# Down projection: 18 of 22 block pairs in the seven-product form, with all their weight sums made ahead and five pairs' activation forms kept in device memory

## The chip, the cores and the metric

The kernel runs on one core of a Trainium2 chip. The metric is device microseconds of one execution. A core has five engines that run side by side, each with its own queue of instructions: TensorE (PE in the profile; its weight loads are PEld), VectorE (DVE), ScalarE (ACT), GpSimd (POOL) and SyncE (SP). They meet at semaphores. Data come from device memory by DMA; a DMA is issued from the queue of SP, ACT or POOL and is then carried by the core's 16 DMA engines. TensorE reads SBUF and adds into PSUM, which VectorE and ScalarE read.

## What is computed

One decoder layer in float32 with 256 tokens and a model width of 2048: a mixer of three kinds of heads, a projection, and a gated feed-forward part with 5632 features. The change touches the last line only, the product with `w_down`:

```python
def conv_glu_ffn(h, w_gate, w_up, conv_w, conv_b, w_down):
    g = h @ w_gate                                  # [256, 5632]
    gp = jnp.pad(g, ((0, 0), (CONV_WIDTH - 1, 0), (0, 0)))
    gc = conv_b
    for j in range(CONV_WIDTH):
        gc = gc + conv_w[j] * gp[:, j:j + S]
    return (jax.nn.silu(gc) * (h @ w_up)) @ w_down  # [256, 5632] @ [5632, 2048]

x = x + conv_glu_ffn(rms_norm(x, g_ffn), w_gate, w_up, conv_w, conv_b, w_down)
```

## The kernel before

**High and low parts.** TensorE multiplies floats rounded to a shorter format (F32R). To keep float32 accuracy every operand is split: ScalarE writes the rounded high part (`wh`, line 101), VectorE the rest (`wl`, line 102), both in `split_w`, into rings of four buffers each. A product is then three matmuls: high x high, low x high, high x low (`prod`, lines 906 to 910).

**Gate and up.** The 5632 features are 44 blocks of 128 (`f`). For each f the loop at line 879 loads one block of `w_gate` and one of `w_up` (1 MB each, line 88, a ring of three buffers named `wr`), splits them and multiplies them with the normed tokens `h2`: 96 matmuls of 256 columns (line 165). `glu` (lines 824 to 854) then makes the gated feature block: convolution, silu, product.

**Down.** Two neighbouring feature blocks are a pair `j`; there are 22. The outputs are computed in two halves `c` of 1024 columns. For a half, a pair of feature blocks, two blocks of 128 tokens and two of 512 columns make a 2 x 2 by 2 x 2 block product. A *plain* pair does it with eight block products, 24 matmuls of 512 columns (`plain`). A *seven* pair uses a scheme with seven block products, 21 matmuls (`seven`): its activations are seven sums of the four blocks, made in `glu` and kept as a tile `aS` of seven high and seven low parts (128 x 14 x 128), and its weights are three blocks and four sums of blocks. Three of the seven products go to accumulators of one output block each (`own`), four to accumulators of common parts (`com`), which `common` and `finish` put together at the end of a half and add to the residual.

**Where the weight sums are made.** `KIND` at line 43 gives each place of the order a letter. "p" is plain (8 of 22). "s" (6) is a seven pair whose sums VectorE makes in down, one pair ahead (`make_sums`, lines 928 to 938). "S" (8) is a seven pair whose sums are made during gate and up: `presum` (lines 859 to 866) loads the four weight blocks through the same ring `wr`, makes four differences on VectorE and stores the result to device memory (`tsum`) from POOL's queue. There are 16 such jobs, one for each half and "S" pair, one behind each odd f from 3 to 33. In down an "S" pair loads three quarters of its weights in two pieces, and 1 MB of sums.

**Queues.** All loads of weights are issued in program order from SP's queue: a load that waits for its buffer holds back those behind it. In down the loads use four places in turn, the ring of three and a part of `dn` (line 900). POOL's queue issues the stores of the sums, the loads of the residual `x1s` into `dn` (line 967) and the first half's output.

Of the kernel before, what the change touches and what calls it, by code (L numbers as in the profile page):

```python
# [18 lines left out]
P = 128  # L19
# [19 lines left out]
NN = 512  # L39

PAIRS = KF // 2
ORDER = tuple(range(PAIRS - 3)) + (PAIRS - 1, PAIRS - 2, PAIRS - 3)
KIND = "pSspSsSpsSpSspSsSpsSpp"
SEVEN = tuple(j for j, k in zip(ORDER, KIND) if k != "p")
SUMMED = tuple((c, j) for c in range(2) for j, k in zip(ORDER, KIND) if k == "S")

VEC = [
    ("g_mix", KD), ("g_ffn", KD), ("g_q_lat", QR // P), ("g_kv_lat", KVR // P),
# [15 lines left out]
def layer(ctx, tc, xT_d, xn_d, memT_d, vec_d, tab_d, w_z_d, w_mqkr_d, w_q_d, w_kv_d, w_mem_d, w_pool_d, w_o_d,  # L64
# [10 lines left out]
    def nm(s):  # L75
        uid[0] += 1
        return f"{s}_{uid[0]}"
# [13 lines left out]
    def keep(ins, on=True):  # L91

        return tc.keep_in_program_order(ins) if on else ins
# [730 lines left out]
    def glu(f, psg, psu, home=None):  # L824
        g = fp.tile([P, T], F32, tag="g", name=nm("g"), bufs=1)
        nc.vector.tensor_tensor(g[:], psg, r1[:], op=ALU.mult)  # L826
        gc = fp.tile([P, T], F32, tag="gc", name=nm("gc"), bufs=1)
        nc.scalar.activation(gc[:], g[:], AF.Identity, bias=v("conv_b", f), scale=v("cw2", f))  # L828
        for d, w in ((1, "cw1"), (2, "cw0")):
            nc.vector.scalar_tensor_tensor(gc[:, d:T], g[:, 0:T - d], v(w, f), gc[:, d:T], op0=ALU.mult, op1=ALU.add)  # L830
        nc.scalar.activation(gc[:], gc[:], AF.Silu)  # L831
        j, e = f // 2, f % 2
        if j not in SEVEN:
            if e == 0:
                aT[j] = fp.tile([P, 2, 2 * T], F32R, name=nm("aT"))
            nc.vector.tensor_tensor(gc[:], psu, gc[:], op=ALU.mult)
            split_act(aT[j][:, e, :], gc[:])
            return
        if e == 0:
            aT[j] = home if j == PAIRS - 1 else fp.tile([P, 14, P], F32R, name=nm("aS"))[:]  # L840
            hold[j] = fp.tile([P, 8, P], F32, tag="s8", name=nm("s8"), bufs=1)
        elif home is not None:
            aT[j] = home
        s = hold[j]
        o = 0 if e else 6
        nc.vector.tensor_tensor(s[:, o:o + 2, :].rearrange("p a t -> p (a t)"), psu, gc[:], op=ALU.mult)
        if e:
            for d, a, op, b in ((2, 7, ALU.add, 1), (3, 2, ALU.subtract, 6), (4, 6, ALU.subtract, 7),
                                (5, 0, ALU.subtract, 3)):
                nc.vector.tensor_tensor(s[:, d, :], s[:, a, :], s[:, b, :], op=op)  # L850
            hi, lo = (aT[j][:, i:i + 7].rearrange("p a t -> p (a t)") for i in (0, 7))
            sf = s[:, 0:7, :].rearrange("p a t -> p (a t)")
            nc.scalar.copy(hi, sf)
            nc.vector.tensor_tensor(lo, sf, hi.bitcast(F32), op=ALU.subtract)


    tsum = dp.tile([P, len(SUMMED), STG], F32, name="tsum")

    def presum(i):

        raw = load_w(w_dn_d[SUMMED[i]], STG)
        r = raw.rearrange("p (b n) -> p b n", n=NN)
        for d, a, b in ((0, 1, 0), (1, 2, 1), (2, 2, 0), (3, 3, 2)):
            nc.vector.tensor_tensor(r[:, d], r[:, a], r[:, b], op=ALU.subtract)  # L864
        for h in range(2):
            nc.gpsimd.dma_start(tsum[:, i, h * HS:(h + 1) * HS], raw[:, h * HS:(h + 1) * HS])  # L866
# [12 lines left out]
    for f in range(1, KF):  # L879
        pss = [ps_main()[:, 0:T] for _ in range(2)]  # L880
        gemm_pair(pss, [load_w(w[f], STG) for w in (w_g_d, w_u_d)], h2)
        if f < KF - 1:
            glu(f, *pss)
        if f % 2 and 3 <= f < 3 + 2 * len(SUMMED):
            presum(f // 2 - 1)

# [5 lines left out]
    dn = big.tile([P, 12, NN], F32, tag="act", name="dn")  # L892
    aS = big.tile([P, 14, P], F32R, tag="act2", name="aS")
    glu(KF - 1, *pss, aS[:])
    cnt = [0, 0]

    def load_dn(src, parts=((0, STG),)):

        cnt[1] += 1
        raw = dn[:, 4:8].rearrange("p b n -> p (b n)") if cnt[1] % 4 == 0 else stage.tile(  # L900
            [P, STG], F32, tag="wr", name=nm("wr"), bufs=3)[:]
        for a, b in parts:
            nc.sync.dma_start(raw[:, a:b], src[:, a:b])
        return raw

    def prod(ps, a, b, first, last):
# [5 lines left out]
    def plain(c, j, own, first, last, kept, between=None, by_bank=False):  # L912
        raw = load_dn(w_dn_d[c, j])
        ws = [split_w(raw, 0, HS, kept=kept)]
        if between is not None:
            between()
        ws.append(split_w(raw, HS, HS, kept=kept))
        order = [(k, t, n) for k in range(2) for t in range(NT) for n in range(2)]
        if by_bank:
            order.sort(key=lambda o: o[1:])  # L920
        for k, t, n in order:
            a = [aT[j][:, k, o + t * P:o + (t + 1) * P] for o in (0, T)]
            s = n if k == 0 else 1 - n
            prod(own[t, n], a, [w[:, s * NN:(s + 1) * NN] for w in ws[k]], first and k == 0, last and k == 1)

    ready = {}

    def make_sums(c, j):

        raw = load_dn(w_dn_d[c, j])  # L930
        r3 = raw.rearrange("p (b n) -> p b n", n=NN)
        i = cnt[0] % 2
        cnt[0] += 1
        f13, f24 = dn[:, 2 * i:2 * i + 2], dn[:, 2 - 2 * i:4 - 2 * i]
        keep(nc.vector.tensor_tensor(f13, r3[:, 1:3], r3[:, 0:2], op=ALU.subtract))
        keep(nc.vector.tensor_tensor(f24[:, 0], r3[:, 2], f13[:, 0], op=ALU.subtract))
        keep(nc.vector.tensor_tensor(f24[:, 1], r3[:, 3], f24[:, 0], op=ALU.subtract))
        ready[c, j] = (raw, *(f.rearrange("p b n -> p (b n)") for f in (f13, f24)))

    def seven(c, j, own, com, first, last, kept, between):  # L940
        if (c, j) in SUMMED:
            raw = load_dn(w_dn_d[c, j], ((0, NN), (2 * NN, STG)))
            sums = load_dn(tsum[:, SUMMED.index((c, j))])
            F13, F24 = sums[:, 0:HS], sums[:, HS:STG]
        else:
            raw, F13, F24 = ready.pop((c, j))
        b11 = split_w(raw, 0, NN, kept=kept)
        b2 = split_w(raw, 2 * NN, HS, kept=kept)
        if between is not None:
            between()  # L950
        t13 = split_w(F13, 0, HS, kept=kept)
        t24 = split_w(F24, 0, HS, kept=kept)
        for (b, s), f, ps, own_ in (((b11, 0), 6, com[0], False), ((b2, 0), 5, own[0, 1], True),
                                    ((b2, 1), 0, own[0, 0], True), ((t13, 0), 2, com[1], False),
                                    ((t13, 1), 4, com[3], False), ((t24, 0), 3, com[2], False),
                                    ((t24, 1), 1, own[1, 0], True)):
            prod(ps, [aT[j][:, i + f, :] for i in (0, 7)], [w[:, s * NN:(s + 1) * NN] for w in b],
                 first and not own_, last and not own_)

    def common(c, com, step):  # L960

        v1, u2, u3, u5 = (dn[:, i, :] for i in range(4))
        if step == 0:
            for t in range(NT):
                for n in range(2):
                    o = c * HS + n * NN
                    nc.gpsimd.dma_start(dn[:, 8 + 2 * t + n, :], x1s[:, t, o:o + NN])
        elif step == 1:
            keep(nc.scalar.copy(v1, com[0]))
            for u, a, b in ((u2, v1, com[2]), (u3, u2, com[3]), (u5, u3, com[1]), (u2, u2, com[1])):  # L970
# [17 lines left out]
    for c in range(2):  # L988
        own_ps, com_ps = (ps_main, ps_aux) if c else (ps_aux, ps_main)
        own = {(t, n): own_ps()[:] for t in range(NT) for n in range(2)}  # L990
        com = None
        for i, j in enumerate(ORDER):
            kept = c > 0 or i > 1
            between = None
            if i == 0 and done is not None:
                between = lambda o=done: finish(0, o, nc.gpsimd)
            elif i >= PAIRS - 2:
                between = lambda s=i - PAIRS + 3: common(c, com, s)
            elif KIND[i + 1] == "s":
                between = lambda j=ORDER[i + 1]: make_sums(c, j)  # L1000
            if j in SEVEN:
                if com is None:
                    com = [com_ps()[:] for _ in range(4)]
                seven(c, j, own, com, j == SEVEN[0], j == SEVEN[-1], kept, between)
# [8 lines left out]
def _pack(**i):  # L1013
# [58 lines left out]
    r["w_u"] = cols(a["w_up"][0])  # L1072

    w = a["w_down"][0].reshape(PAIRS, 2, P, 2, 2, NN)
    w = np.stack([w[:, 0, :, :, 0], w[:, 0, :, :, 1], w[:, 1, :, :, 1], w[:, 1, :, :, 0]])
    r["w_dn"] = w.transpose(3, 1, 2, 0, 4).reshape(2, PAIRS, P, STG)
    return {n: np.ascontiguousarray(x, dtype=f32) for n, x in r.items()}

# [16 lines left out]
```

## Time and profile before

| | us |
|---|---|
| median of three runs | 998.13 (998.0 to 998.34) |
| the profiled execution | 998.5 |
| its span, first to last instruction | 996.7 |

The profile is of one execution. "Busy" is the time in which an engine had an instruction under way; matmuls are pipelined, so a busy TensorE is not TensorE at its peak. A row of a group of instructions gives the line, the engine, the operation, output<-input by the program's names, the shape, the count, then busy time and the mean ns of one, and the idle time just before them with what ended it. The chain of work that ended last is followed back from the last instruction, at each step to what released it. The granted TensorE clock was 1.00 of full speed throughout.

### The profile page before, as it was taken

The page shows a single profiled execution, that of the slowest core. Times are in us where ns is not written, and L with a number is a line of the kernel's source. Part 1 is how long each engine was busy: PE and PEld are TensorE (multiplying, and loading weights), DVE is VectorE, ACT ScalarE, POOL GpSimd, SP SyncE. Part 2 cuts the span into 40 slices and gives each one's busy share as a digit, 9 for nine tenths or more (in the row PEclk, how much of TensorE's full clock was granted, in tenths as well). Part 3 has the DMA queues.
Part 4 walks back from the last instruction along what each step waited for, and adds up shares of the span by engine and source line. Part 5 has one row for each costly group of instructions (what it writes and reads, how often), then busy time and mean ns, then how long its engine had stood idle before and what let it go on. Part 6 is the DMA issues. An engine that isn't in the chain of part 4 may idle for free.

```text
span 996.7 us, 17150 instructions
## 1 busy us (share of the span) xinstructions
PE 989.7 (99%) x6888; PEld 917.2 (92%) x6888; DVE 757.3 (76%) x1117; ACT 566.2 (57%) x770; POOL 35.5 (4%) x71
## 2 busy tenths in 40 slices
PE   9999999999999999999999999999999999999998
PEld 8899988888889999999999999999999888887886
DVE  6878588765676777777786777876656988898897
ACT  6777665644565554554554455455544666655663
POOL 1100000000000000000000000000000000010000
PEclk9999999999999999999999999999999999999999
DMA  9867445344665888887888887785656877787772
GB/s 359 291 245 287 137 161 178 127 144 145 211 219 190 298 291 296 296 278 288 281 304 291 295 302 276 281 286 182 208 185 207 300 280 273 266 300 284 283 267 102
DMA packets 43296, 246.51 MB, mean 247 GB/s; under 512 B 4944, under 2 KB 5456, under 8 KB 19280
## 3 DMA queue, kind: packets, MB, share of 16 engines
q1 hardware_dynamic: 35424, 218.41, 62.3%
q0 software_dynamic: 7360, 26.22, 6.9%
q8 instruction: 54, 0.88, 0.3%
q10 hardware_dynamic: 432, 0.79, 0.3%
q14 instruction: 26, 0.21, 0.1%
HBM read 224.42 MB, written 20.97 MB: 246 GB/s over the span
## 4 chain that ended last, share of the span: by engine, by line
PE 97%; DVE 1%; ACT 1%; issue 0%; ACTq 0%; DVEq 0%
PE psm L165 47%; PE psm L181 5%; PE psm L182 5%; PE psm L183 5%; PE psm L148 4%; PE psa L910 4%; PE psa L908 4%; PE psa L909 4%; PE psm L908 4%; PE psm L910 4%; PE psm L909 4%; PE psm L132 2%; PE psa L713 1%; PE psa L181 1%; PE psa L183 1%; PE psa L182 1%
## 5 line engine op out<-in xcount | busy, mean ns | idle before, releaser
L102 DVE TENSOR_TENSOR wl<-wr,wh 128x1024 fp32r<-128x1024 f32 (+2 forms) x362 | 419.5, 1168 | 166.7 <-ACT wh L101 110.9
L101 ACT CAST wh<-wr 128x1024 fp32r<-128x1024 f32 (+2 forms) x362 | 362.5, 1006 | 200.5 <-PE psm L165 83.0
L165 PE MATMUL psm<-h,wh 128*128 128x256 f32 x2752 | 319.1, 276 | 0.0
L165 PEld LDWEIGHTS psm<-h,wh 128*128 128x128 f32 x2752 | 315.3, 188 | 0.0
L165 PE MATMUL psm<-h,wl 128*128 128x256 f32 x1376 | 163.0, 276 | 0.0
L165 PEld LDWEIGHTS psm<-h,wl 128*128 128x128 f32 x1376 | 159.2, 188 | 0.0
L101 ACT CAST wh<-dn 128x1024 fp32r<-128x1024 f32 (+1 forms) x54 | 52.6, 974 | 33.3 <-PE psa L909 19.3
L102 DVE TENSOR_TENSOR wl<-dn,wh 128x1024 fp32r<-128x1024 f32 (+1 forms) x54 | 59.6, 1124 | 8.9 <-ACT wh L101 6.9
L828 ACT ACTIVATE gc<-g,vec 128x256 f32<-128x256 f32 x44 | 26.5, 602 | 70.0 <-DVE g L826 70.0
L831 ACT ACTIVATE gc<-gc 128x256 f32<-128x256 f32 x44 | 18.4, 418 | 70.5 <-DVE gc L830 70.5
L864 DVE TENSOR_TENSOR wr<-wr 128x512 f32<-128x512 f32 x64 | 44.1, 689 | 1.1
L830 DVE SCALAR_TENSOR_TENSOR gc<-g,vec,gc 128x255 f32<-128x255 f32 x88 | 42.3, 480 | 1.0
L910 PE MATMUL psa<-wl,aS 128*128 128x512 f32 x98 | 38.4, 392 | 0.9 <-DVE wl L102 0.9
L908 PE MATMUL psa<-wh,aS 128*128 128x512 f32 x98 | 38.2, 389 | 0.0
L909 PE MATMUL psa<-wh,aS 128*128 128x512 f32 x98 | 38.2, 389 | 0.0
L908 PE MATMUL psm<-wh,aS 128*128 128x512 f32 x98 | 38.1, 389 | 0.0
L909 PE MATMUL psm<-wh,aS 128*128 128x512 f32 x98 | 38.1, 389 | 0.0
L910 PE MATMUL psm<-wl,aS 128*128 128x512 f32 x98 | 38.1, 389 | 0.0
L181 PE MATMUL psm<-wh,cat 128*128 128x512 f32 x96 | 38.1, 397 | 0.0
L183 PE MATMUL psm<-wl,cat 128*128 128x512 f32 x96 | 37.4, 390 | 0.0
L182 PE MATMUL psm<-wh,cat 128*128 128x512 f32 x96 | 37.4, 390 | 0.0
L866 POOL DMA_DIRECT2D tsum<-wr x32 | 17.0, 533 | 344.5 <-DVE wr L864 344.5
(233 smaller groups left out, 1362.0 us busy)
## 6 DMA issues: line engine op xcount, KB each, us to landing
wr<-in_w_g SPq DMA_DIRECT2D x44, 1024.0 KB, 5.0
wr<-in_w_u SPq DMA_DIRECT2D x44, 1024.0 KB, 5.5
wr<-in_w_dn SPq DMA_DIRECT2D x37, 1024.0 KB, 5.1
wr<-in_w_o SPq DMA_DIRECT2D x16, 1024.0 KB, 4.9
tsum<-wr POOLq DMA_DIRECT2D x32, 512.0 KB, 4.0
wr<-tsum SPq DMA_DIRECT2D x12, 1024.0 KB, 6.1
wr<-in_w_z SPq DMA_DIRECT2D x10, 1024.0 KB, 6.0
dn<-in_w_dn SPq DMA_DIRECT2D x7, 1024.0 KB, 6.6
```

Source lines behind the costliest of these rows:

```text
L101: keep(nc.scalar.copy(hi[:, c:e], raw[:, o + c:o + e]), kept)
L102: keep(nc.vector.tensor_tensor(lo[:, c:e], raw[:, o + c:o + e], hi[:, c:e].bitcast(F32), op=ALU.subtract), kept)
L148: keep(nc.tensor.matmul(ps, parts[k // nk][low][:, i * P:(i + 1) * P], m, start=k + a == 0 and low == low_first, stop=k == KD - 1 and low ...
L165: nc.tensor.matmul(ps, parts[k // nk][low][:, i * P:(i + 1) * P], m, start=k + a == 0 and low == (s == 1), stop=k == KD - 1 and low == (s ...
L181: keep(nc.tensor.matmul(ps, xh, hi[:, i, o], start=first and i == 0, stop=False), kept)
L182: keep(nc.tensor.matmul(ps, xl, hi[:, i, o], start=False, stop=False), kept)
L183: keep(nc.tensor.matmul(ps, xh, lo[:, i, o], start=False, stop=last and i == nk - 1), kept)
L830: nc.vector.scalar_tensor_tensor(gc[:, d:T], g[:, 0:T - d], v(w, f), gc[:, d:T], op0=ALU.mult, op1=ALU.add)
L864: nc.vector.tensor_tensor(r[:, d], r[:, a], r[:, b], op=ALU.subtract)
L908: nc.tensor.matmul(ps, a[0], b[0], start=first, stop=False)
L909: nc.tensor.matmul(ps, a[1], b[0], start=False, stop=False)
L910: nc.tensor.matmul(ps, a[0], b[1], start=False, stop=last)
```

## The change

The order of the 22 pairs is written out, and only pairs 0, 8, 14 and 15 stay plain. The other 18 are seven pairs, and all of them are summed ahead: 36 jobs instead of 16, spread over f = 2 to 40, one behind each f but 11, 21 and 31 (none). The jobs load into two places of their own (`wj`) instead of the ring `wr`. `make_sums` and `KIND` are gone.

The forms of pairs 16 to 20 (`AWAY`) are not kept in SBUF. They are made in one place (`aL`), stored to device memory (`forms`) from POOL's queue, and in each half loaded back into that one place, one after the other: the next load is issued behind the pair that used the place.

In down the loads go through six places in turn: the three of `wr`, the two of `wj` and the part of `dn`. The first and second weight blocks of a pair are exchanged in the packed weights, so that a seven pair's three blocks are one piece of 768 KB; the signs of two sums and the order of two products follow. The residual's loads move from POOL's queue to SP's, and a plain pair's second block order changes likewise.

```diff
-ORDER = tuple(range(PAIRS - 3)) + (PAIRS - 1, PAIRS - 2, PAIRS - 3)
-KIND = "pSspSsSpsSpSspSsSpsSpp"
-SEVEN = tuple(j for j, k in zip(ORDER, KIND) if k != "p")
-SUMMED = tuple((c, j) for c in range(2) for j, k in zip(ORDER, KIND) if k == "S")
+ORDER = (0, 1, 16, 2, 3, 4, 17, 5, 6, 7, 18, 8, 9, 10, 19, 11, 12, 21, 20, 13, 14, 15)
+PLAIN = (0, 8, 14, 15)
+AWAY = (16, 17, 18, 19, 20)
+SEVEN = tuple(j for j in ORDER if j not in PLAIN)
+SUMMED = tuple((c, j) for c in range(2) for j in SEVEN)
...
-            aT[j] = home if j == PAIRS - 1 else fp.tile([P, 14, P], F32R, name=nm("aS"))[:]
+            aT[j] = (home if j == PAIRS - 1 else away() if j in AWAY
+                     else fp.tile([P, 14, P], F32R, name=nm("aS"))[:])
...
             nc.vector.tensor_tensor(lo, sf, hi.bitcast(F32), op=ALU.subtract)
+            if j in AWAY:
+                nc.gpsimd.dma_start(forms[:, AWAY.index(j)], aT[j])
+
+    forms = dp.tile([P, len(AWAY), 14, P], F32R, name="forms")
+
+    def away():
+        return fp.tile([P, 14, P], F32R, tag="aL", name=nm("aL"), bufs=1)[:]
...
+    def job_place():
+        return fp.tile([P, STG], F32, tag="wj", name=nm("wj"), bufs=2)[:]
...
     def presum(i):
-        raw = load_w(w_dn_d[SUMMED[i]], STG)
+        c, j = SUMMED[i]
+        raw = job_place()
+        nc.sync.dma_start(raw, w_dn_d[c, j])
         r = raw.rearrange("p (b n) -> p b n", n=NN)
-        for d, a, b in ((0, 1, 0), (1, 2, 1), (2, 2, 0), (3, 3, 2)):
+        for d, a, b in ((1, 0, 1), (0, 2, 0), (2, 2, 1), (3, 3, 2)):
...
-        if f % 2 and 3 <= f < 3 + 2 * len(SUMMED):
-            presum(f // 2 - 1)
+        for i in range(len(SUMMED)):
+            if f == 2 + i * (KF - 4) // len(SUMMED):
+                presum(i)
...
+    def load_dn(src, a=0):
+        cnt[0] += 1
+        n = cnt[0] % 6
+        raw = (dn[:, 4:8].rearrange("p b n -> p (b n)") if n == 0 else job_place() if n % 3 == 1
+               else stage.tile([P, STG], F32, tag="wr", name=nm("wr"), bufs=3)[:])
+        nc.sync.dma_start(raw[:, a:STG], src[:, a:STG])
+        return raw
...
+    def fetch(j):
+        aT[j] = away()
+        nc.gpsimd.dma_start(aT[j], forms[:, AWAY.index(j)])
+
+    def seven(c, j, own, com, first, last, kept):
+        raw = load_dn(w_dn_d[c, j], NN)
+        sums = load_dn(tsum[:, SUMMED.index((c, j))])
+        b11 = split_w(raw, NN, NN, kept=kept)
         b2 = split_w(raw, 2 * NN, HS, kept=kept)
+        t31 = split_w(sums, 0, HS, kept=kept)
+        t24 = split_w(sums, HS, HS, kept=kept)
...
-                    nc.gpsimd.dma_start(dn[:, 8 + 2 * t + n, :], x1s[:, t, o:o + NN])
+                    nc.sync.dma_start(dn[:, 8 + 2 * t + n, :], x1s[:, t, o:o + NN])
...
+        rest = [j for j in ORDER if j in AWAY]
+        fetch(rest.pop(0))
         for i, j in enumerate(ORDER):
...
+                seven(c, j, own, com, j == SEVEN[0], j == SEVEN[-1], kept)
+                if j in AWAY and rest:
+                    fetch(rest.pop(0))
...
-    w = np.stack([w[:, 0, :, :, 0], w[:, 0, :, :, 1], w[:, 1, :, :, 1], w[:, 1, :, :, 0]])
+    w = np.stack([w[:, 0, :, :, 1], w[:, 0, :, :, 0], w[:, 1, :, :, 1], w[:, 1, :, :, 0]])
```

More of the change, by code (lines that the diff above doesn't have):

```diff
@@ L894, in layer @@
     glu(KF - 1, *pss, aS[:])
[L895 to L903, printed above, removed]
+    cnt = [0]
+    def load_dn(src, a=0):
[4 more added lines that the diff above has]
+        nc.sync.dma_start(raw[:, a:STG], src[:, a:STG])
         return raw
@@ L922, in plain @@
             a = [aT[j][:, k, o + t * P:o + (t + 1) * P] for o in (0, T)]
-            s = n if k == 0 else 1 - n
+            s = 1 - n
             prod(own[t, n], a, [w[:, s * NN:(s + 1) * NN] for w in ws[k]], first and k == 0, last and k == 1)
[L926 to L947, printed above, removed]
+    def fetch(j):
[5 more added lines that the diff above has]
+        b11 = split_w(raw, NN, NN, kept=kept)
         b2 = split_w(raw, 2 * NN, HS, kept=kept)
[L949 to L952, printed above, removed]
+        t31 = split_w(sums, 0, HS, kept=kept)
+        t24 = split_w(sums, HS, HS, kept=kept)
         for (b, s), f, ps, own_ in (((b11, 0), 6, com[0], False), ((b2, 0), 5, own[0, 1], True),
-                                    ((b2, 1), 0, own[0, 0], True), ((t13, 0), 2, com[1], False),
-                                    ((t13, 1), 4, com[3], False), ((t24, 0), 3, com[2], False),
+                                    ((b2, 1), 0, own[0, 0], True), ((t31, 1), 2, com[1], False),
+                                    ((t31, 0), 4, com[3], False), ((t24, 0), 3, com[2], False),
                                     ((t24, 1), 1, own[1, 0], True)):
@@ L991, in layer @@
         com = None
+        rest = [j for j in ORDER if j in AWAY]
+        fetch(rest.pop(0))
         for i, j in enumerate(ORDER):
             kept = c > 0 or i > 1
[L994 to L1000, printed above, removed]
             if j in SEVEN:
@@ L1003, in layer @@
                     com = [com_ps()[:] for _ in range(4)]
-                seven(c, j, own, com, j == SEVEN[0], j == SEVEN[-1], kept, between)
-            else:
+                seven(c, j, own, com, j == SEVEN[0], j == SEVEN[-1], kept)
+                if j in AWAY and rest:
+                    fetch(rest.pop(0))
+            else:
+                between = None
+                if i == 0 and done is not None:
+                    between = lambda o=done: finish(0, o, nc.gpsimd)
+                elif i >= PAIRS - 2:
+                    between = lambda s=i - PAIRS + 3: common(c, com, s)
                 plain(c, j, own, i == 0, i == PAIRS - 1, kept, between, i == PAIRS - 1)
```

## The prediction

> **What bounds the kernel now.** I read the page's totals first, then its chain of work that ended last, then a table of the stages.
>
> ```profile
> span 996.7 us, 17150 instructions
> PE 989.7 (99%) x6888; PEld 917.2 (92%) x6888; DVE 757.3 (76%) x1117; ACT 566.2 (57%) x770; POOL 35.5 (4%) x71
> ...
> PE 97%; DVE 1%; ACT 1%; issue 0%; ACTq 0%; DVEq 0%
> ```
>
> The chain is TensorE for 97%: only fewer or shorter matmuls can gain, and only as long as nothing else becomes late. The table of stretches (start:end, length, busy us and instruction counts of PE, PEld, DVE, ACT, POOL, then clock, DMA share, GB/s) covers the first loads, gate and up with sums, gate and up without, and down:
>
> ```profile
> 4.00:32.00 28.00, 28.00 (x122) 23.10 (x121) 22.21 (x33) 21.95 (x35) 1.33 (x3) 1.00 1.03 410
> 324.00:650.00 326.00, 326.00 (x2879) 326.00 (x2878) 249.60 (x363) 166.51 (x199) 15.79 (x30) 1.00 0.81 290
> 673.00:747.00 74.00, 74.00 (x655) 74.00 (x655) 46.84 (x65) 37.53 (x48) 0.00 (x0) 1.00 0.56 190
> 770.20:990.90 220.70, 219.79 (x969) 181.18 (x968) 196.72 (x203) 135.62 (x144) 6.34 (x12) 1.00 0.75 265
> ```
>
> Three readings. In down one 512-column matmul costs 219.79/969 = 0.2268 us, and TensorE hardly ever waits. VectorE is at 89% there and 77% in gate and up. The DMA engines move 265 and 290 GB/s, while the first row shows 28 us at 410: that is what they can do when there is always work queued, so about a third is free, and the change will use it.
>
> **The change part by part.** *Matmuls.* A plain pair issues 24 matmuls (two k, two t, two n, three products of high and low parts), a seven pair 7 x 3 = 21. Four pairs in each of two halves change: 8 x 3 = 24 fewer, 24 x 0.2268 = **5.44 us** less. They are on the chain, so this is the whole possible gain but for TensorE's own wait in down, one row:
>
> ```profile
> PE psa L910 <- DVE wl L102: 0.9, 1, 0.9
> ```
>
> *VectorE in down.* The sums of the six "s" pairs in each half leave down. The rows of that stage by shape:
>
> ```profile
> L102 DVE TENSOR_TENSOR wl<-wr,wh 128x1024 fp32r<-128x1024 f32 x70 | 84.2, 1221 | 5.2 <-ACT wh L101 3.9
> L102 DVE TENSOR_TENSOR wl<-wr,wh 128x512 fp32r<-128x512 f32 x17 | 11.6, 685 | 0.0
> L935 DVE TENSOR_TENSOR dn<-wr 128x1024 f32<-128x1024 f32 x6 | 7.3, 1222 | 3.1 <-DMA wr<-in_w_dn 3.1
> L936 DVE TENSOR_TENSOR dn<-wr,dn 128x512 f32<-128x512 f32 x6 | 4.2, 692 | 0.2
> ```
>
> A seven pair's splits cost 3 x 1.221 + 0.685 = 4.35 us of VectorE against 21 x 0.2268 = 4.76 us of TensorE. The 1.22 + 2 x 0.69 = 2.6 us of sums go from twelve pairs, and eight pairs gain 4.35 - 2.44 = 1.9 us each: 31 us out, 15 in. VectorE keeps 91% of a seven pair's time, as now on average, so I cost this at nothing; its cover is the 0.4 us left in each pair, which repays lateness only slowly.
>
> *VectorE in gate and up.* 36 jobs instead of 16, each four of the first row below; before, one in every second feature block f, now one in each f from 2 to 40 except 11, 21 and 31.
>
> ```profile
> L864 DVE TENSOR_TENSOR wr<-wr 128x512 f32<-128x512 f32 x64 | 44.1, 689 | 1.1
> L850 DVE TENSOR_TENSOR s<-s 128x128 f32<-128x128 f32 x53 | 15.4, 291 | 1.4
> L854 DVE TENSOR_TENSOR aS<-s,aS 128x896 fp32r<-128x896 f32 x13 | 14.2, 1093 | 13.2 <-ACT aS L853 13.2
> ...
> 415.93 1.23 DVE L102 TENSOR_TENSOR wl<-wr,wh 128x1024 fp32r<-128x1024 f32 x1 [1.55 <-PE psm L165]
> ```
>
> The row without jobs has 46.84/74 = 63% of VectorE; a job is 2.76 us of the 10.88 us that one f takes, another 25%, and the forms of more pairs 1 or 2%: about 90%. What now falls on the odd f, a job and the end of a pair's forms together, is already in the trace, and there VectorE still idles 1.55 us for TensorE (last line). The change gives the even f a job without the forms. I cost it at nothing too; if the cover goes, each f pays its own tenths, 39 times.
>
> *DMA in gate and up.* The period comes from the timeline of TensorE, and what is loaded or stored from the page's DMA issues (KB each, median us to landing):
>
> ```profile
> 407.51 7.42 PE L165 MATMUL psm<-h,wh 128*128 128x256 f32 x64
> 414.77 3.79 PE L165 MATMUL psm<-h,wl 128*128 128x256 f32 x32
> 418.39 5.83 PE L165 MATMUL psm<-h,wh 128*128 128x256 f32 x50
> ...
> wr<-in_w_g SPq DMA_DIRECT2D x44, 1024.0 KB, 5.0
> tsum<-wr POOLq DMA_DIRECT2D x32, 512.0 KB, 4.0
> wr<-tsum SPq DMA_DIRECT2D x12, 1024.0 KB, 6.1
> wr<-in_w_dn SPq DMA_DIRECT2D x12, 512.0 KB, 4.7
> dn<-x1s POOLq DMA_DIRECT2D x8, 256.0 KB, 7.0
> wr<-in_w_dn SPq DMA_DIRECT2D x12, 256.0 KB, 3.7
> ```
>
> One f is 418.39 - 407.51 = 10.88 us. Two weight blocks are 2.10 MB, a job loads 1.05 and stores 1.05: 4.19 MB, **386 GB/s** wherever a job lies. Over f 32 to 40 four stores of forms (128 x 14 x 128 x 4 bytes = 0.92 MB) come on top: 41.4 MB in 97.9 us, 423 GB/s. The capacity with such a mix, in short stretches of the same table where loads overlap stores (first two rows) and in down (third):
>
> ```profile
> 432.00:436.00 4.00, 4.00 (x38) 4.00 (x37) 3.93 (x6) 2.82 (x3) 1.06 (x2) 1.00 0.98 405
> 455.00:459.00 4.00, 4.00 (x38) 4.00 (x37) 2.92 (x4) 2.78 (x4) 0.53 (x1) 1.00 1.04 372
> 795.00:799.00 4.00, 4.00 (x19) 3.31 (x18) 3.57 (x4) 2.92 (x5) 0.00 (x0) 1.00 0.99 401
> ```
>
> I take 405, near three of the four rows. Then f 2 to 31 just fit (37.7 MB of nine f take 93.2 of 97.9 us) and f 32 to 40 end 41.4/0.405 - 97.9 = 4.3 us late. What covers that is in the queue's timeline:
>
> ```profile
> 408.03 0.33 SPq L88 DMA_DIRECT2D wr<-in_w_g  x1
> ...
> 418.65 0.33 SPq L88 DMA_DIRECT2D wr<-in_w_u  x1
> ...
> 413.46 1.05 ACT L101 CAST wh<-wr 128x1024 fp32r<-128x1024 f32 x1 [1.07 <-DMA wr<-in_w_g]
> ...
> SPq L88 <- DMA tsum<-wr: 24.2, 16, 2.6
> ```
>
> A gate block cast at 413.46 is multiplied from 418.39 + 32 x 0.113 = 422.0: 8.5 us of lead, even where the cast itself waited 1.07 us for the load. The job's own two places (not the weights' ring, as before) take away a wait of the last line's kind, but put another in: SP's load of job i+2 waits for the stores of job i, and the next gate and up loads stand behind it. From VectorE's job end to the next load is some 1 + 4 us, while the job two f later comes 21.8 us on, so this fits. POOL's queue gets 40 more stores, five stores and ten fetches of forms of the 0.53 us that one costs its issuer; it was 4% busy. Cost of the stage: from 0 (405 and all of the lead) to 41.4/0.372 - 97.9 = 13 us less some 6 of lead = 7; I take 1.
>
> *DMA in down.* A seven pair loads 768 KB of blocks and 1,024 KB of sums, 1.835 MB in 4.76 us. One half: 18 x 1.835 + 4 x 1.049 + five forms at 0.92 + 1.05 of residual (its four loads move from POOL's queue into SP's, where they add four issues ahead of the next weights) = 42.9 MB, against 30.4 now. Five of six places and the first forms, 5.6 MB, can be filled before down begins; the first half's output writes 1.05. Left are 2 x 42.9 + 1.05 - 5.6 = 81.1 MB, and they must have landed some 8 us (a plain pair's 5.4 and the first split's 2.3) before the last of 948 x 0.2268 = 215.0 us of matmuls: 81.1/207 = **392 GB/s**. At 401 to 410 it fits with 2 to 4% to spare, at 372 it takes 218 + 8 - 215 = 11 us more. I take 0.5 us.
>
> *Forms fetched.* No row shows a transfer of rounded floats between device memory and SBUF. The single place is free when the last matmul of its pair is done, and the next such pair starts three pairs, 14.3 us, later. The nearest row is four residual loads of 256 KB by POOL's queue beside SP's loads, 7.0 us. At 7 to 10 us it is hidden; that is the value I take. At 20 us each would hold TensorE for some 6 us, ten times.
>
> The sum is made on the profiled execution's 998.5 us (span 996.7 and 1.8 around it): 998.5 - 5.4 + 1.0 + 0.5 = 994.6; the median shown is 0.4 lower, so **994.2**.
>
> A rule of the Trainium skill speaks against this. "DMA: Bandwidth & Descriptors", section Bandwidth, holds that some 358 GB/s of a core's share of device memory binds for loads into SBUF; the "HBM Reference" limits that to both cores of a pair streaming and gives about 425 for one alone. This trace's 410 over 28 us sides with the second.
>
> **The rivals.** *The engines fall short in down (slower).* Mixed sizes, stores and fetches could bring the sustained rate to 380; it decides from 392 down, and beats the gain from 382. Down: 81.1/0.380 + 8 - 215 = 6.4 us; f 32 to 40: 41.4/0.380 - 97.9 = 11, less 6 of lead, 5. 998.1 - 5.4 + 11.4 = 1004. For it: the row of 372, and no stretch over 28 us at 400. Against it: that row holds the start of a transfer after a pause, which a full queue does not have.
>
> *The gain is given back in gate and up alone.* With VectorE at 90% and loads at 96%, a late job load holds VectorE's queue, behind it the low parts. Some 0.1 us in each of 39 f, or the whole 4.3 us of f 32 to 40: 998.
>
> *The forms come late (slower).* As above, six us ten times less the cover: 1040.
>
> *A steady 358 GB/s.* Gate and up from f 2 to 40 would move 161 MB in 450 instead of 424 us, 26 less 6 of lead; down 81.1/0.358 + 8 - 215 = 20 us: 998.1 - 5.4 + 20 + 20 = 1033. The 410 row excludes it nearly. It is the first page's rule above.
>
> That the change does not do what it says can hardly be: the matmuls are counted by the code.
>
> **How the numbers follow.** The forecast with its own range 992 to 996: 0.57, all faster by over 0.2%, which is 2 us and about what a measurement of this kernel can tell from no change. Gain given back: 0.16, within 0.2%. Engines short: 0.20, late forms 0.05, steady 358 0.02, together 0.27 slower. The range goes from 991.8 (no cost, and TensorE's old wait gone) to 1005, which leaves out the last two, a little of the third and the lowest tail, some 0.15.
>
> **What would show it.** The count of 512-column matmuls falls by 24 with their spacing still 0.227 us. Right: gate and up still takes 10.88 us an f, GB/s near 386 there and 395 in down, and TensorE's waits stay under 2 us. Wrong: ScalarE's casts waiting for loads of weights, jobs or sums by many us, TensorE waiting for wh or wl in f 32 to 40 or in the runs of seven pairs, the DMA share at 1.0 with less than 390 GB/s, or matmuls of pairs 16 to 20 waiting for aL.

## The result, and the profile after

| | median us | range | runs |
|---|---|---|---|
| before | 998.07 | 997.88 to 998.34 | 4 |
| changed | 1087.79 | 1086.77 to 1089.96 | 4 |

The ratio of the changed kernel to the one before is 1.0901, 95% interval 1.0888 to 1.0914: 89.7 us slower, far outside the range. The profiled execution took 1088.4 us. Its page, first the totals, then the chain that ended last by engine and by line, then the DMA issues (KB each, median us to landing):

```profile
span 1086.6 us, 17440 instructions
PE 1013.1 (93%) x6864; PEld 936.8 (86%) x6864; DVE 797.9 (73%) x1189; ACT 572.9 (53%) x782; POOL 60.6 (6%) x118
...
PE 64%; DMA 22%; DVE 10%; issue 2%; ACT 1%; DVEq 0%; SPq 0%; ACTq 0%
...
wr<-in_w_g SPq DMA_DIRECT2D x44, 1024.0 KB, 7.5
wr<-in_w_u SPq DMA_DIRECT2D x44, 1024.0 KB, 8.0
wj<-in_w_dn SPq DMA_DIRECT2D x40, 1024.0 KB, 6.5
tsum<-wj POOLq DMA_DIRECT2D x72, 512.0 KB, 7.4
```

6,864 matmuls are the 24 fewer that were counted. But the chain, 97% TensorE before, is now 64% TensorE, 22% DMA and 10% VectorE, a gate load lands in 7.5 us instead of 5.0, and half a job's store in 7.4 instead of 4.0. Where this happens is read from the table of stretches of the changed kernel (columns as in the prediction; the last row is down):

```profile
324.00:420.00 96.00, 80.15 (x635) 79.16 (x635) 70.69 (x108) 35.65 (x44) 10.13 (x19) 0.91 0.92 341
420.00:530.00 110.00, 83.76 (x672) 82.16 (x671) 73.24 (x111) 36.74 (x45) 11.22 (x21) 0.89 0.91 333
530.00:640.00 110.00, 90.18 (x699) 88.50 (x700) 82.00 (x123) 39.10 (x49) 11.73 (x22) 0.88 0.94 353
640.00:770.00 130.00, 125.67 (x1088) 124.87 (x1087) 88.39 (x128) 63.00 (x77) 3.74 (x7) 0.99 0.75 263
770.00:866.00 96.00, 96.00 (x850) 96.00 (x849) 63.51 (x91) 48.90 (x57) 2.67 (x5) 1.00 0.70 239
866.20:1081.50 215.30, 215.25 (x949) 177.47 (x947) 185.28 (x184) 147.57 (x160) 6.99 (x13) 1.00 0.94 374
```

Down is as forecast: 215 us, 0.2268 us a matmul, no waits of TensorE. Everything is lost in gate and up, and there in the first 340 us: DMA share 0.91 to 0.94, only 333 to 353 GB/s, a lower clock, and VectorE at 67 to 75%, no fuller than before. From f 1 to 43, the same 4,128 matmuls, before:

```profile
302.00:770.00 468.00, 468.00 (x4131) 468.00 (x4130) 342.26 (x492) 239.36 (x289) 17.05 (x32) 1.00 0.75 264
```

and after:

```profile
302.00:866.00 564.00, 497.76 (x4128) 492.69 (x4127) 394.53 (x583) 233.55 (x285) 41.64 (x78) 0.94 0.84 306
```

564 - 468 = 96 us: 66 us in which TensorE stood, and 30 us by which the same matmuls took longer. The first part has its names in the waits (us in total, times, longest):

```profile
DVE wj L878 <- DMA wj<-in_w_dn: 88.8, 28, 6.2
...
PE psm L166 <- DVE wl L103: 66.2, 24, 6.6
```

TensorE waits for low parts, VectorE for jobs' loads. And SP's own queue, whose waits of this kind summed to 24.2 us before:

```profile
SPq L875 <- DMA tsum<-wj: 248.1, 34, 11.3
```

One turn of it, first SP's queue (start, us), where L875 is a job's load and L89 a gate (g) or up (u) load:

```profile
440.80 0.33 SPq L89 DMA_DIRECT2D wr<-in_w_g  x1
451.37 0.33 SPq L875 DMA_DIRECT2D wj<-in_w_dn  x1
452.13 0.33 SPq L89 DMA_DIRECT2D wr<-in_w_u  x1
452.57 0.36 SPq L89 DMA_DIRECT2D wr<-in_w_g  x1
462.00 0.33 SPq L875 DMA_DIRECT2D wj<-in_w_dn  x1
462.42 0.38 SPq L89 DMA_DIRECT2D wr<-in_w_u  x1
473.41 0.33 SPq L875 DMA_DIRECT2D wj<-in_w_dn  x1
```

SP is silent from 441 to 451, 453 to 462 and 463 to 473. The chain (start, us) says for what:

```profile
443.41 7.81 DMA tsum<-wj
451.37 5.30 DMA wj<-in_w_dn
...
463.09 10.18 DMA tsum<-wj
473.41 5.70 DMA wj<-in_w_dn
```

The load at 451.37 goes out when the last store from its place has landed, and the u load of 452.13 stood behind it. VectorE then passes the lateness on, since it too works in order:

```profile
469.42 0.69 DVE L878 TENSOR_TENSOR wj<-wj 128x512 f32<-128x512 f32 x1 [4.13 <-DMA wj<-in_w_dn]
470.03 0.28 DVE L852 TENSOR_TENSOR s<-s 128x128 f32<-128x128 f32 x1
470.23 1.22 DVE L103 TENSOR_TENSOR wl<-wr,wh 128x1024 fp32r<-128x1024 f32 x1
```

A difference waits 4.13 us for the load issued at 462.00; behind it is a split whose result TensorE takes at 471.50, after a pause of 5.28 us.

Last, how dense the jobs are. SP's queue in this stretch alternates "g J u g J u J" (J is a job's load), three jobs for two gate loads, where the code has one job behind each f. The 36 job loads went out between 297.7 and 659.0 us. From 302 to 629 us POOL issued 62 half stores, 31 jobs, while TensorE did 2,158 matmuls of line 166, 22.5 f: 1.38 jobs an f. At 10.88 us an f that is (2.10 + 1.38 x 2.10) MB, **459 GB/s**, not 386. So the build of the kernel does not keep the written order of a queue; only instructions given to `keep` stay behind the one written before them on their engine. That weights are loaded "in program order", as the section on the kernel before has it, is true of that kernel's queue ("g u g u J" over and over) but no rule. There the jobs shared the ring `wr` with the weights, which would hold each job's load in its place; with places of their own the jobs moved ahead. Experiment 2 puts them back into the ring.

The theories taken to the chip: (A) the jobs stand too dense, and one in each f costs nothing; (B) the stores cost even then, because SP's load of job i+2 waits for the stores of job i with weights behind it, or because the DMA engines cannot carry the rate; (C) VectorE is too full.

### The profile page after: what moved, and what is told of

Its sections match the earlier page's. It is cut to its first block, busy times and chain, and to the rows that moved or that the text cites. A ratio compares the mean times of both kernels' runs of the same rounds, so it can differ in the third digit from the quotient of the medians.

```text
span 1086.6 us, 17440 instructions
## 1 busy us (share of the span) xinstructions
PE 1013.1 (93%) x6864; PEld 936.8 (86%) x6864; DVE 797.9 (73%) x1189; ACT 572.9 (53%) x782; POOL 60.6 (6%) x118
## 4 chain that ended last, share of the span: by engine, by line
PE 64%; DMA 22%; DVE 10%; issue 2%; ACT 1%; DVEq 0%; SPq 0%; ACTq 0%
PE psm L166 19%; DMA tsum<-wj 12%; DMA wj<-in_w_dn 10%; PE psm L182 5%; PE psm L184 5%; PE psm L183 5%; DVE wj L878 4%; DVE wl L103 4%; PE psm L149 4%; PE psa L923 3%; PE psa L925 3%; PE psa L924 3%; PE psm L923 3%; PE psm L924 3%; PE psm L925 3%
## 5 line engine op out<-in xcount | busy, mean ns | idle before, releaser
L102 ACT CAST wh<-wr 128x1024 fp32r<-128x1024 f32 (+2 forms) x352 | 346.4, 1003 | 142.5 <-PE psm L183 51.2
L166 PE MATMUL psm<-h,wh 128*128 128x256 f32 x2752 | 331.9, 282 | 0.0
L166 PEld LDWEIGHTS psm<-h,wh 128*128 128x128 f32 x2752 | 329.0, 194 | 0.0
L166 PE MATMUL psm<-h,wl 128*128 128x256 f32 x1376 | 180.7, 288 | 66.2 <-DVE wl L103 66.2
L166 PEld LDWEIGHTS psm<-h,wl 128*128 128x128 f32 x1376 | 170.8, 197 | 71.3 <-DVE wl L103 71.3
L878 DVE TENSOR_TENSOR wj<-wj 128x512 f32<-128x512 f32 x144 | 99.2, 689 | 90.8 <-DMA wj<-in_w_dn 88.8
L103 DVE TENSOR_TENSOR wl<-wj,wh 128x1024 fp32r<-128x1024 f32 (+1 forms) x54 | 60.0, 1114 | 12.3 <-ACT wh L102 7.4
L102 ACT CAST wh<-wj 128x1024 fp32r<-128x1024 f32 (+1 forms) x54 | 51.8, 965 | 22.0 <-PE psm L924 11.5
L880 POOL DMA_DIRECT2D tsum<-wj x72 | 38.4, 534 | 343.6 <-DVE wj L878 241.2
L855 ACT CAST aS<-s 128x896 fp32r<-128x896 f32 x13 | 12.2, 941 | 60.6 <-DVE s L852 60.6
```

Source lines behind the costliest of these rows:

```text
L102: keep(nc.scalar.copy(hi[:, c:e], raw[:, o + c:o + e]), kept)
L103: keep(nc.vector.tensor_tensor(lo[:, c:e], raw[:, o + c:o + e], hi[:, c:e].bitcast(F32), op=ALU.subtract), kept)
L166: nc.tensor.matmul(ps, parts[k // nk][low][:, i * P:(i + 1) * P], m, start=k + a == 0 and low == (s == 1), stop=k == KD - 1 and low == (s ...
```

## The experiments

All times are medians beside runs of the kernel before on the same chip (998.0 to 998.2 throughout); the interval is that of the ratio to it.

**1. Is it the stores at all, or VectorE?** Two kernels without the jobs' stores, one job in each f and three in two f; the differences are held in written order by `keep`.

```diff
-            nc.vector.tensor_tensor(r[:, d], r[:, a], r[:, b], op=ALU.subtract)
+            keep(nc.vector.tensor_tensor(r[:, d], r[:, a], r[:, b], op=ALU.subtract))
-        for h in range(2):
-            nc.gpsimd.dma_start(tsum[:, i, h * HS:(h + 1) * HS], raw[:, h * HS:(h + 1) * HS])
...
-        sums = load_dn(tsum[:, SUMMED.index((c, j))])
+        sums = load_dn(w_dn_d[c, j])
```

The dense one (three jobs in two f, by `f == 2 + i * 2 // 3`):

> As e6, but the jobs' sums are not stored, and down loads weight blocks of the same size in their place, so the output leaves out the right sums. VectorE's work is the same, the DMA's need in gate and up falls to 2.1 + 1.5 x 1.05 = 3.7 MB in 10.88 us, 337 GB/s, and a place is free when VectorE is done. Theory A: 992 to 1010. Theory C: stays over 1050.

The sparse one:

> As e1, but the jobs' sums are not stored and down loads weight blocks of the same size in their place, so the output leaves out the right sums. One job behind each f, VectorE's work unchanged, the DMA's need 290 GB/s. S and D both: 991 to 995, the forecast's 994 without its DMA terms. If VectorE at 90% costs anything by itself: above 997.

Measured: sparse **993.1** us, ratio 0.9948 (0.9929 to 0.9968); dense 1000.2, 1.0025 (1.0015 to 1.0036). The sparse one's stretch:

```profile
324.00:640.00 316.00, 316.00 (x2790) 316.00 (x2790) 272.07 (x406) 160.20 (x192) 0.00 (x0) 1.00 0.77 282
```

VectorE is at 86% with all 36 jobs and TensorE never stands. So (C) falls, and the matmuls and down give 5.0 of the 5.4 us forecast. Even 1.5 jobs an f cost only 7 us without stores. Both lie in the expected ranges.

**2. Density.** The same `keep`, with the stores; then the same with three jobs in two f; and the jobs put back into the ring `wr` (`raw = load_w(w_dn_d[c, j], STG)`), with nothing held.

> The changed kernel, with VectorE's four differences of every job held at their place in the written order, one job behind each f. Theory A (the jobs were issued far ahead of their place, three in two f, which asks the DMA engines for 2.1 + 1.5 x 2.1 = 5.2 MB in 10.88 us, 482 GB/s, so that every job's load waits for stores two jobs back and VectorE's queue, and behind it TensorE, for the load): 992 to 998, gate and up back at 468 to 473 us, no TensorE wait over 2 us for wl. Theory B (two places are too few at any density: load 6, VectorE 6, stores 10 us, 22 us for two jobs, 11 us a job, against 10.88 us an f): 1015 to 1050. Theory C (VectorE is too full with a job in each f): 1030 or more, with VectorE's share near 95% and no waits of VectorE for job loads.

> As e1, but the written order itself puts three jobs behind every two f (f = 2 to 25). Theory A: 1075 to 1095, as the changed kernel, for the order of issue is nearly its order. If the density were harmless and the planner's fine placing the trouble: below 1030.

> The changed kernel, with the jobs loaded through the weights' ring of three again, which holds them at their place, one in each f. Theory A: far better than 1088, but the job takes a place that the weights need until its stores land, three loads for three places in 10.88 us: 1000 to 1040. Theory B (only two places of its own were the trouble): 995 to 1005. Theory C: 1030 or more.

Measured: 1039.7 (1.0403, 1.0381 to 1.0424); dense 1092.5 (1.0946, 1.0924 to 1.0968); ring 1065.1 (1.0679, 1.0644 to 1.0714). From 324 to 640 us, one job in each f:

```profile
324.00:640.00 316.00, 300.82 (x2550) 296.63 (x2548) 246.68 (x370) 140.48 (x173) 25.63 (x48) 0.98 0.88 326
```

and three in two:

```profile
324.00:640.00 316.00, 258.42 (x2062) 254.49 (x2060) 225.32 (x339) 110.70 (x135) 33.10 (x62) 0.92 0.90 339
```

Density on purpose gives the changed kernel's time (1087.8), and written order takes 48 us of it away. (A) is shown as a cause, but not as the only one: 42 us above before remain with one job in each f: the 992 to 998 of the first text was missed, and its 1015 to 1050, two places too few even so, was met. With the ring the queue reads "g u J", one job in each f, so it is the ring that held the jobs in place. But a ring of three for 88 weight blocks and 36 jobs is no cure: 25 us above theory A's range. The text's theory C, 1030 or more, would hold the time, but (C) fell in experiment 1.

**3. What remains: where the job's load stands, the number of places, the size of a store.** All on the first kernel of 2. Loads from POOL's queue instead of SP's:

```diff
-        nc.sync.dma_start(raw, w_dn_d[c, j])
+        nc.gpsimd.dma_start(raw, w_dn_d[c, j])
```

> As e1, but the jobs' loads are issued from POOL's queue, so that no load of gate or up weights stands behind a job's load that waits for stores. Theory S (the weights are late because SP's queue stands still: 186 us of SP's waits in e1 are for stores of jobs): 992 to 1008. Theory D (with stores in the mix the DMA engines cannot carry 386 GB/s, they gave 320 to 357 in e1): 1030 to 1045.

1064.7 us (1.0665, 1.0644 to 1.0686), worse. POOL's job loads now wait 378.5 us for stores, with the next job's stores behind them, and VectorE waits 71.6 us for job loads: the same stand in another queue. Both expected ranges were missed, so the run does not decide between the two theories.

Four places instead of two (`bufs=4`; pairs 3, 4 and 5 write into pair 2's tile of forms, `aT[j - 1] if j in (3, 4, 5)`):

> As e1, but with four places for jobs instead of two; the SBUF for them comes from pairs 3, 4 and 5 sharing the tile of forms of pair 2, so the output leaves out these pairs' own forms. A job's load no longer waits for stores two jobs back but four. The bytes are the same. Theory S: 992 to 1008. Theory D: 1025 to 1045.

1032.2 us (1.0357, 1.0316 to 1.0398): 8 us better, and SP still waits 177.5 us for stores (186 in the first kernel of 2). The time lies in theory D's range; but the wait that was to go did not go, so this does not speak against S. Why it stayed was not followed.

One store of 1 MB for a job (`nc.gpsimd.dma_start(tsum[:, i], raw)`), in the kernel of 2 and in the changed kernel:

> As e1, with one store of 1,024 KB (8 KB rows) for each job instead of two of 512 KB (4 KB rows). Theory S: about 1040, or a little more, since the first half's store starts later. Theory D with the row size as its reason: below 1020. D without it: within 5 us of e1.

> The changed kernel with nothing held, only the one store of 8 KB rows for each job. If the density of the jobs (three in two f, 482 GB/s) is the larger half of the loss whatever the rows: 1055 to 1075, the 25 to 35 us of e10 against e1 saved here too. If the rows explain nearly all: below 1020.

1005.4 (1.0087, 1.0057 to 1.0118) and 1049.5 (1.0522, 1.0480 to 1.0564), 34 and 38 us better, the second by 6 us more than expected at best. It looked like the size of a row in memory. But one store also changes what the build arranges, so the next three have all of SP's loads in gate and up held in written order, g, u, job: with two stores, with one, and with one into a block of its own (`tsum` as [36, P, STG]).

```diff
-            nc.sync.dma_start(raw[:, c:min(n, c + cut)], src[:, c:min(n, c + cut)])
+            keep(nc.sync.dma_start(raw[:, c:min(n, c + cut)], src[:, c:min(n, c + cut)]), fpo[0])
...
-        nc.sync.dma_start(raw, w_dn_d[c, j])
+        keep(nc.sync.dma_start(raw, w_dn_d[c, j]))
...
+    fpo[0] = True
     for f in range(1, KF):
```

> As e1, and every load of SP's queue in gate and up held in the written order too (gate, up, job, gate, up, job), with the jobs' two stores of 512 KB. It is the control for e13. If the planner's order of SP's loads was what e10 gained by: 1000 to 1012. If it was the rows of the stores: within 10 us of e1's 1040.

> As e12, the same order of SP's loads, but one store of 1,024 KB in 8 KB rows for each job. If the rows of the stores matter: 20 to 35 us below e12, about 1000 to 1010. If only the order did: within 5 us of e12.

> As e13, with each job's sums in one stretch of 1 MB in device memory instead of rows 288 KB apart. If the spacing of the rows costs the stores something: 3 to 10 us below e13. If not: within 3 us of e13.

1074.6 (1.0775, 1.0756 to 1.0795), 1079.2 (1.0825, 1.0794 to 1.0856), 1076.0 (1.0788, 1.0769 to 1.0807). With the order fixed, one store gains nothing, and neither does the layout (3 us, intervals overlap). So the 34 us were most likely those of an order; which of its displacements did it was not tried. And the written order is much worse than the build's, which none of the texts expected: the first of the three lies 25 us above the higher of its ranges. Its SP queue, with one store, first the wait, in the view of the queue's waits:

```profile
SPq L876 <- DMA tsum<-wj: 388.0, 34, 15.5
```

then the timeline:

```profile
505.75 0.33 SPq L876 DMA_DIRECT2D wj<-in_w_dn  x1
506.17 0.38 SPq L90 DMA_DIRECT2D wr<-in_w_g  x1
506.64 0.38 SPq L90 DMA_DIRECT2D wr<-in_w_u  x1
520.06 0.33 SPq L876 DMA_DIRECT2D wj<-in_w_dn  x1
```

After each job load, g and u go out at once: both were long due, and stood behind the job's load. SP stands for 13 us, until the stores of two jobs ago have landed, and one f takes 14 us instead of 10.9. Here (B) is seen plainly, but not which of its two reasons.

**4. The job's load where its place is already free.** The load of a job behind the gate load of the next f, one weight block later, and its differences ahead of `glu` of its f. All of SP's loads are held as in 3.

```diff
+    g_next = load_w(w_g_d[1], STG)
     for f in range(1, KF):
         pss = [ps_main()[:, 0:T] for _ in range(2)]
-        gemm_pair(pss, [load_w(w[f], STG) for w in (w_g_d, w_u_d)], h2)
+        raws = [g_next, load_w(w_u_d[f], STG)]
+        if f < KF - 1:
+            g_next = load_w(w_g_d[f + 1], STG)
+        due = [i for i in range(len(SUMMED)) if f == 2 + i * (KF - 4) // len(SUMMED)]
+        jobs = [(i, job_load(i)) for i in due]
+        gemm_pair(pss, raws, h2)
+        for job in jobs:
+            presum(*job)
         if f < KF - 1:
             glu(f, *pss)
```

Two stores, one store, two stores with the differences behind `glu` again, and the first without stores:

> One job in each f, all of SP's loads held in the written order, in which a job's load now stands behind the gate load of the next f, and its differences on VectorE stand ahead of the elementwise work of this f; two stores per job. Theory 1 (SP waits at the job's load for stores two jobs back, and weights wait behind it): when SP comes to the load, the stores are some 10 us old or more, SP's waits for stores of the sums fall from 382 us to under 60 and the time to 993 to 1000. Theory 2 (the DMA engines cannot carry 386 GB/s with stores in it): loads of gate and up still land late, above 1005.

> The same order with one store of 1 MB per job. Theory 1: the same time as with two stores within 3 us, 993 to 1000. Theory 2: above 1005; if the size of a row in memory matters after all, this one is faster than the one with two stores by over 5 us.

> The same order of loads with two stores, but the differences of a job behind the elementwise work of its f, some 5 us later. Theory 1: the stores then land some 5 us later against the same place in SP's queue, so SP waits more and the time lies above the run with the differences ahead, by 3 to 40 us. Theory 2: no difference over 3 us between the two.

> The same order of loads and differences without the stores of the sums; down loads blocks of the down weights of the same size in their place, so the output is not the reference's. Both theories: 992 to 995, as the run without stores before it (993.1); if it is above 998, the order itself costs something and the two runs with stores have to be read against this one.

Measured: two stores **1007.9** (1.0092, 1.0065 to 1.0119); one store 1004.1 (1.0055, 1.0031 to 1.0079); differences behind `glu` **1055.9** (1.0576, 1.0543 to 1.0609); without stores 995.4 (0.9970, 0.9959 to 0.9980). SP's wait for stores, differences ahead:

```profile
SPq L875 <- DMA tsum<-wj: 86.8, 27, 8.7
```

and behind:

```profile
SPq L875 <- DMA tsum<-wj: 299.2, 34, 15.4
```

The same loads in the same order in SP's queue and the same stores, only the differences later in VectorE's: 48 us. VectorE's order alone is not the reason, since without stores the differences behind `glu` cost nothing (993.1 in experiment 1). Against the written order of 3 with two stores (1074.6) the moved load by itself gives 19 us. With the differences ahead the stretch reads

```profile
324.00:640.00 316.00, 314.23 (x2756) 313.04 (x2755) 266.72 (x395) 151.74 (x187) 27.68 (x52) 1.00 0.97 362
```

against 281 GB/s at a share of 0.78 without stores. 362 GB/s are carried with TensorE at 99%: so of (B) the stand in SP's queue is shown, and the DMA rate as the cause of the large loss falls. Theory 1 was not met in full, though: its range up to 1000 was missed by 8 and 4 us, the wait that was to fall under 60 us was 86.8 with two stores, and the differences behind `glu` cost more than the 40 us that it allowed.

**5. What is left.** Two changes of the kernel with one store: the jobs in f 2 to 37 without a pause (`f == 2 + i`), to keep their last stores off down's first loads; and four places, made as in 3.

> As the run with the moved load and one store (1004.1), with the 36 jobs in f 2 to 37 without a pause, so that three f are left to the loads of down. If the end of the jobs is what is left (a), 995 to 1000 and below before. If the rate is (c), the pauses were needed: SP falls behind steadily and the time is 1004 or more. If the places are (b), 1002 to 1006.

> As the run with the moved load and one store (1004.1), with four places for the jobs; to make room pairs 3, 4 and 5 use the tile of pair 2's forms, so that their own forms are left out and the output is not the reference's. If the two places are what is left (b), SP waits for no store and the time is 995 to 998. If the rate of the DMA engines is (c), 1002 to 1006, with no waits of SP for the stores but loads of gate and up that land late. If the end of the jobs is (a), 1000 to 1004.

Measured: 1014.0 (1.0150, 1.0135 to 1.0164) and 1000.9 (1.0034, 1.0023 to 1.0045). Without the three pauses it is 10 us slower. That refutes (a) as it was put, and fits both a cycle that catches up in the pauses and (c). With four places the time lies in the range of (a), between those of (b) and (c), and SP waits for no store at a job's load. The stretches:

```profile
324.00:640.00 316.00, 316.00 (x2790) 316.00 (x2790) 273.20 (x404) 158.00 (x192) 13.84 (x26) 1.00 0.97 368
...
700.00:770.00 70.00, 67.35 (x577) 66.04 (x576) 54.20 (x81) 32.06 (x40) 3.73 (x7) 1.00 1.01 396
```

and, from the same order without stores:

```profile
700.00:770.00 70.00, 70.00 (x620) 70.00 (x619) 55.51 (x82) 35.23 (x42) 2.13 (x4) 1.00 0.88 316
```

From 324 to 640 us nothing is lost at 368 GB/s. From 700 to 770, where the last jobs, the forms' stores and the first loads of down fall together, the DMA share is 1.01, and TensorE does 43 matmuls fewer, 43 x 0.113 = 4.9 us: most of the 5.4 us between the two kernels. So what is left stands mostly there, where the DMA engines have no share free.

| step, each from the kernel above it | us | difference |
|---|---|---|
| changed kernel | 1087.8 | |
| one job in each f (differences held) | 1039.7 | -48 |
| load one block later, differences ahead of `glu`, all of SP's loads held | 1007.9 | -32 |
| one store | 1004.1 | -4, intervals overlap |
| four places (forms of three pairs left out) | 1000.9 | -3, intervals overlap |
| no stores (two places) | 995.4 | -5 |
| loads in the build's order, differences behind `glu` | 993.1 | -2, intervals overlap |

No complete version beat the kernel before; the best is 1004.1 us.

## Why the prediction was wrong

*Matmuls, -5.44 us: right.* 24 fewer, still 0.2268 us each; without stores the kernel gains 5.0 us.

*VectorE in down and in gate and up, nothing: right.* TensorE stood nowhere in down, and 86% in gate and up left no wait in experiment 1. VectorE had the time; in the changed kernel it passed on the lateness of the jobs' loads because it works in order.

*DMA in down, 0.5 us, at 392 GB/s: right.* 215 us, and in the middle of it the changed kernel's table has

```profile
900.00:960.00 60.00, 60.00 (x267) 49.67 (x266) 51.52 (x49) 44.77 (x49) 2.12 (x4) 1.00 1.02 419
```

419 GB/s over 60 us, which settles the rival of a steady 358 and, for down, that of short engines. On the average down took only 374 GB/s, less than the 392 that the prediction asked for.

*Forms fetched, hidden at 7 to 10 us: right.* Issues of the changed kernel:

```profile
aL<-forms POOLq DMA_DIRECT2D x10, 896.0 KB, 9.4
```

*DMA in gate and up, 1 us with bounds 0 and 7: wrong, 96 us.* Three statements failed, in this order of weight.

"Now one in each f from 2 to 40": that is where the code has the jobs. The trace has 1.38 in each f up to f 23. In the kernel before the place of a job's load was fixed by the shared ring, and the prediction took away the ring without asking what else held the load. 48 us, by holding the differences.

"From VectorE's job end to the next load is some 1 + 4 us, while the job two f later comes 21.8 us on, so this fits": the 4 us were the landing time in the trace of before, at 290 GB/s. In the changed kernel, at 333 to 353 GB/s, a half store lands in 7.4. And the 21.8 us are counted between VectorE's jobs, while SP asks for the place well before: it runs ahead of TensorE by the ring's three blocks, so that its load of job i+2 comes when the differences of job i may be just done. The statement named the wait and the weights behind it, and then sized it with an unloaded landing time at the wrong point of the queue. 32 us, by moving the load with its differences; 48 us are lost again when the differences alone stand later in VectorE's queue. The likely reason, which no run isolates, is that late weights delay the job that frees the place.

"I take 405": where stores were in the mix, 368 GB/s came with a share of 0.97 and 396 with 1.01, that is 380 to 392 at full share, by an estimate that scales the rate with the share. The prediction's own working for f 32 to 40, 41.4 MB, then gives 41.4/0.386 - 97.9 = 9 us less some 6 of lead, 3; some 5 were measured. This term was right in its mechanism and small in size. Its rate was too high: the rival of short engines had 380 for f 32 to 40, and 5 us.

Of the rivals, "the gain is given back in gate and up alone" had the right mechanism (a late job load holds VectorE's queue, behind it the low parts) but 0.1 us in each f instead of 2. No rival had SP's queue as its place, and none had a job's place in the order as unknown.

## What to carry to other kernels

Giving a transfer buffers of its own also removes the order that the shared buffers imposed: read in the changed kernel's queue where its instructions will stand, and pin them if it matters. A load into a place that a store must first leave is a wait in the issuing queue; size it with the landing time under the new load, from the moment the queue reaches the load, not from the moment the data are needed, and count what stands behind it. A few microseconds of slack in such a cycle were worth 48 here, presumably since a late turn makes the next one late.

## What the runs showed of the hardware that was not expected

About a quarter of the loss is TensorE's clock. The table of the changed kernel in steps of 4 us:

```profile
460.00:464.00 4.00, 3.88 (x35) 3.68 (x33) 3.06 (x6) 2.08 (x4) 0.53 (x1) 1.00 1.01 395
464.00:468.00 4.00, 1.21 (x8) 1.00 (x8) 1.29 (x2) 1.59 (x2) 0.00 (x0) 1.00 0.94 330
468.00:472.00 4.00, 0.50 (x2) 0.50 (x3) 2.58 (x5) 0.00 (x0) 0.00 (x0) 0.60 0.79 306
472.00:476.00 4.00, 4.00 (x22) 4.00 (x22) 3.97 (x7) 2.49 (x3) 1.07 (x2) 0.55 0.63 205
476.00:480.00 4.00, 4.00 (x36) 4.00 (x35) 2.92 (x6) 1.73 (x3) 0.00 (x0) 1.00 0.99 344
```

and its TensorE timeline (start, us):

```profile
454.65 7.42 PE L166 MATMUL psm<-h,wh 128*128 128x256 f32 x64
...
465.01 1.21 PE L166 MATMUL psm<-h,wl 128*128 128x256 f32 x8 [1.13 <-DVE wl L103]
471.50 2.08 PE L166 MATMUL psm<-h,wl 128*128 128x256 f32 x8 [5.28 <-DVE wl L103]
473.38 8.65 PE L166 MATMUL psm<-h,wh 128*128 128x256 f32 x64
...
631.87 1.48 PE L166 MATMUL psm<-h,wl 128*128 128x256 f32 x8 [2.47 <-DVE wl L103]
634.60 2.07 PE L166 MATMUL psm<-h,wl 128*128 128x256 f32 x8 [1.25 <-DVE wl L103]
```

After a pause of 5.28 us the granted clock is low for some 4 us of work (0.55 to 0.60 in these rows; in steps of 1 us it is 0.50 from 469 to 475): eight matmuls take 2.08 instead of 1.21 us and the next 64 take 8.65 instead of 7.42, 2.1 us on top of the pause. After the pause of 1.13 us the clock stays at 1.00. Behind each of the eight pauses of 3.18 us and more the first eight matmuls take 1.93 to 2.08 us; behind the shorter ones some do too, as behind the one of 1.25 us that stands close behind one of 2.47. Over gate and up, TensorE's busy time times the part of the clock that is missing, in steps of 1 us, sums to 24 of the 30 us by which the matmuls took longer. The Trainium skill has this in "TensorE: Matmul & The Clock Gate", Part 1: an idle window of about 3.4 us halves the clock, and as long a busy one restores it. For single pauses the trace agrees, with 5.28 us against 1.13; the slow matmuls after 1.25 us show that the length of the last pause alone does not decide it here.

Also: stores of 1 MB into rows 288 KB apart took no more of the kernel's time than into one block (1079.2 and 1076.0 us, overlapping intervals; they landed in 8.9 and 8.2 us), and the rounded floats, 896 KB, were read back in 9.4 us.
